# Level products of a gated linear attention: from whole chunks to diagonal blocks in column groups

## The chip, the cores and the metric

One Trainium2 chip, one of its NeuronCores. The metric is the device time of one execution in microseconds (us), lower is better. The kernel computes a whole inference step of a small trunk, and the change touches one part of it, the linear attention.

## The reference, cut to what matters

Layer 0 mixes tokens by bidirectional gated linear attention with 4 heads, 128 key and 256 value channels per head. Within a chunk it is

```python
bcum  = jnp.cumsum(gi, axis=2)                                   # log decay, per token and key channel
diff  = bcum[:, :, :, None, :] - bcum[:, :, None, :, :]
decay = jnp.exp(jnp.where(lower[:, :, None], diff, -jnp.inf))
attn  = jnp.einsum('bhik,bhjk,bhijk->bhij', qi, ki, decay)       # the decay depends on i, j and the channel k
o     = jnp.einsum('bhij,bhjv->bhiv', attn, vi) + ...            # plus the part read from the state
```

once forwards and once on the flipped sequence; the two results are added. There are 1024 latent and 128 context tokens. Around it stand projections, an output projection, a convolutional MLP, and a second layer with Fourier mixing.

## The kernel before, in words

Channels lie on the 128 partitions, the 1152 tokens along the free dimension. The kernel works in chunks of 128 tokens, nine of them, and takes three at a time: 384 columns, here called a **chunk group**. Heads are taken one after the other, and within a head the chunk groups from the last to the first, so `attention` (line 485) runs its loop body (lines 509 to 592) 12 times.

The decay of a pair of tokens depends on the channel, so one product cannot give `attn`. The kernel splits a chunk into **levels** (`LEVELS`, 64 down to 1). At level s the chunk is cut in blocks of 2s tokens, and the product covers pairs whose two tokens lie in different halves of one block, with the decay measured from the middle of the block. For each level POOL and DVE subtract (lines 535 and 537, tile `le`), ACT takes the exponential (540, 544), POOL multiplies with k (541), DVE with q (546), TensorE forms a full product of 128 x 128 for each of the three chunks (549, PSUM tile `lv`), and DVE copies the pairs of this level out of it under a mask (551) into the tile `A`. The pairs of a token with itself come first (527, 528). With the diagonal that makes 24 full products for a chunk group, 288 in all. `A` then goes into the product with v (line 565), which starts the output `o`; after it come the squares and the normalisation (`os`, `ov`, lines 573 to 582).

All these operands are plain fp32: one product stands in the trace as two records, each with its own weight load. The big projections (`pq`, `pk`, `pv`, `pr` for q, k, v and the output gate r, and `wo`, line 621, for the output projection) are split into two fp32r parts and take three records of 256 or 384 columns (lines 97 to 99).

What sets the order: a tile scheduler orders the instructions of each engine ahead of time, by priorities and by its own idea of durations. Each engine then runs its list strictly in that order. While a head's attention runs, the projections of the next head fill TensorE; at the last head there is no next one, and the output projection of heads 0 and 1 (`w_out`) fills instead. `tick` (line 193) puts small pieces of a background job in between, the modulation vectors (`mod_background`, line 175, tile `mods`): products with only 32 stationary columns, four of them side by side in the array's four column groups through `tile_position`. The tiles `le` come from a ring of four buffers, so the levels of the next chunk group are made ahead until the ring is full.

Of the kernel before, what the change touches and what calls it, by code (L numbers as in the profile page):

```python
# [15 lines left out]
F32 = mybir.dt.float32  # L16
# [29 lines left out]
def trunk(tc, a, o):  # L46
# [15 lines left out]
    def t30(name, dt=F32):  # L62
        return sb.tile([P, 2, CH], dt, tag="m3", bufs=4, name=name)
# [4 lines left out]
    def at_ps(name):  # L68
        return pp.tile([P, 512], F32, tag="at", bufs=4, name=name)
# [32 lines left out]
    def const(name, shape, dt=F32, src=None):  # L102
        t = con.tile(shape, dt, name=name)
        if src is not None:
            nc.sync.dma_start(t, src)
        return t
# [273 lines left out]
    gng = const("gng", [P, 2], src=a["gng"])  # L380
    convw = const("convw", [P, 2, 3, NF], src=a["convw"])
    convb = const("convb", [P, 2, NF], src=a["convb"])
    mask = const("mask", [P, len(LEVELS), P], U8)
    mraw = sb.tile([P, 1032], F32, tag="wr", bufs=2, name="mraw")
    nc.sync.dma_start(mraw[:, :len(LEVELS) * P], a["mask"])
    V.tensor_copy(mask.rearrange("p l i -> p (l i)"), mraw[:, :len(LEVELS) * P])
    for ch in range(NCH):
        ev_glr(ch, pss[ch])

# [89 lines left out]
    def kv(kt, v, c):  # L479
# [2 lines left out]
                  start=True, stop=True)  # L482
        return ps

    def attention(h, qk, pages):

        dec = sb.tile([P, 2, 9], F32, tag="dec", bufs=2, name="dec")
# [21 lines left out]
        for cg in (2, 1, 0):  # L509
# [11 lines left out]
                    sbs[c - 1] = s_n  # L521

            att = t15("A")
            ps = at_ps("lv")
            for c in range(3):
                s = cg * CH + c * P
                PE.matmul(ps[:, c * P:(c + 1) * P], lhsT=qk[:, s:s + P], rhs=qk[:, T + s:T + s + P], start=True, stop=True)
            S.activation(att, ps[:, :CH], AF.Copy, scale=2.0)
            for li, s in enumerate(LEVELS):
                nb = CH // (2 * s)  # L530
                base = cg * CH
                e = t30("le")
                ref = view(bb, s - 1, [2 * s, nb], [CH + 1, 2], [0, s])
                if s > 1:
                    G.tensor_tensor(view(e, 0, [2 * s, nb], [s, 2], [1, s]), ref,  # L535
                                    view(bb, 0, [2 * s, nb], [CH + s, 2], [1, s]), op=ALU.subtract)
                V.tensor_tensor(view(e, CH + s, [2 * s, nb], [-s, 2], [1, s]),
                                view(bb, s, [2 * s, nb], [CH - s, 2], [1, s]), ref, op=ALU.subtract)
                if s > 1:
                    S.activation(e, e, AF.Exp, scale=1.0 / TAU)  # L540
                    G.tensor_tensor(e[:, 0], e[:, 0], qk[:, base:base + CH], op=ALU.mult)  # L541
                    kk, kb = e, 0
                else:
                    S.activation(e[:, 1], e[:, 1], AF.Exp, scale=1.0 / TAU)
                    kk, kb = qk, base
                V.tensor_tensor(e[:, 1], e[:, 1], qk[:, T + base:T + base + CH], op=ALU.mult)
                ps = at_ps("lv")
                for c in range(3):
                    PE.matmul(ps[:, c * P:(c + 1) * P], lhsT=view(kk, kb + c * P, [1, P]),  # L549
                              rhs=e[:, 1, c * P:(c + 1) * P], start=True, stop=True)  # L550
                ins = V.copy_predicated(att.rearrange("p (c i) -> p c i", i=P),
                                  mask[:, li, None, :].to_broadcast([P, 3, P]),
                                  ps[:, :CH].rearrange("p (c i) -> p c i", i=P))
                if li % 2 == 0:
                    tick(1, behind=ins)
            qb = t30("qb")
            S.activation(qb, bb.rearrange("p (z i) -> p z i", z=2), AF.Exp, scale=1.0 / TAU)
            V.tensor_tensor(qb, qb, view(qk, T + cg * CH, [0, 2], [1, CH]), op=ALU.mult)
# [999 lines left out]
```

## Time and profile before

| | |
|---|---|
| median of 3 runs (lowest to highest) | 2561.12 us (2558.16 to 2563.42) |
| the profiled execution, its own time | 2564.86 us |
| its span, first to last instruction | 2563.0 us |
| TensorE, matmuls | 2425.1 us busy, 95% |
| VectorE (DVE) | 1841.2 us busy, 72% |
| ScalarE (ACT) | 1089.3 us busy, 43% |
| GpSimd (POOL) | 730.9 us busy, 29% |
| granted TensorE clock, mean | 0.981 of 2.4 GHz |

The attention lies in the first quarter, from about 60 to 660 us. A record of a matmul in the trace is longer than the time that it takes from the next one, since matmuls are pipelined: what counts is the spacing of starts. A granted clock of 1.00 in a row is 2.4 GHz, 0.50 is 1.2 GHz.

### The profile page before, as it was taken

The numbers are of one execution on the slowest core, as the hardware profiler recorded it, in microseconds if no ns is written. First come the engines' busy times: TensorE is split into PE (matmuls) and PEld (weight loads), VectorE is DVE, ScalarE is ACT, GpSimd is POOL, SyncE is SP. The second block draws the span as 40 slices with busy tenths as digits, with TensorE's granted clock in tenths as the row PEclk, the third lists the DMA queues.
The fourth block names the chain that finished last, engine by engine and source line by source line (L and its number), as shares of the span: only waits on it lengthen the run. The fifth ranks groups of instructions, "written<-read, shape, count | busy, mean of one in ns | idle before, by whom it ended". The sixth has DMA issues, their size and how long they took to land. (4 is left out here: it accounts for less than half of the span.)

```text
span 2563.0 us, 46543 instructions
## 1 busy us (share of the span) xinstructions
PE 2425.1 (95%) x18122; PEld 2329.2 (91%) x18122; DVE 1841.2 (72%) x3339; ACT 1089.3 (43%) x2086; POOL 730.9 (29%) x548
## 2 busy tenths in 40 slices
PE   5999999987999999999999998999899999999997
PEld 4998988877999999999999996998899999999997
DVE  7647475566699677777787877277987778778676
ACT  5435344445364323333345564344533333334553
POOL 3435454453202333444100005230144444410000
PEclk8999999998999999999999999999999999999999
DMA  7212222204233453232674357344223232267334
GB/s 263 69 54 89 80 80 82 67 21 146 87 116 124 132 172 104 91 96 83 212 248 135 112 153 216 107 156 144 90 87 117 83 96 87 80 229 224 93 86 125
DMA packets 200972, 309.85 MB, mean 121 GB/s; under 512 B 18288, under 2 KB 142064, under 8 KB 200752
## 3 DMA queue, kind: packets, MB, share of 16 engines
q1 hardware_dynamic: 196528, 302.66, 37.2%
q10 hardware_dynamic: 4224, 4.23, 0.5%
q8 instruction: 142, 2.33, 0.4%
q14 instruction: 78, 0.64, 0.1%
HBM read 233.71 MB, written 73.11 MB: 120 GB/s over the span
## 5 line engine op out<-in xcount | busy, mean ns | idle before, releaser
L98 PE MATMUL pd<-hl,wd 128*128 128x288 f32 x1112 | 328.7, 299 | 5.4 <-DVE hl L1085 5.2
L99 PE MATMUL pd<-hh,wd 128*128 128x288 f32 x1112 | 326.7, 297 | 0.0
L97 PE MATMUL pd<-hh,wd 128*128 128x288 f32 x1112 | 316.5, 298 | 5.5 <-ACT hh L1084 3.2
L809 POOL TENSOR_TENSOR s<-wa,s 128x512 fp32r<-128x512 f32 x114 | 157.0, 1377 | 278.6 <-ACT s L808 278.6
L1084 ACT ACTIVATE hh<-hr 128x288 fp32r<-128x288 f32 x308 | 133.2, 437 | 222.1 <-PE pd L98 213.3
L98 PEld LDWEIGHTS pd<-hl,wd 128*128 128x128 f32 x1112 | 210.8, 190 | 7.9 <-DVE hl L1085 7.4
L1085 DVE TENSOR_TENSOR hl<-hr,hh 128x288 fp32r<-128x288 f32 x308 | 138.5, 455 | 109.3 <-ACT hh L1084 108.7
L97 PEld LDWEIGHTS pd<-hh,wd 128*128 128x128 f32 x1112 | 204.2, 188 | 10.8 <-ACT hh L1084 5.7
L99 PEld LDWEIGHTS pd<-hh,wd 128*128 128x128 f32 x1112 | 210.4, 190 | 0.0
L809 POOL TENSOR_TENSOR a<-wa,a 128x512 fp32r<-128x512 f32 x76 | 100.1, 1318 | 334.7 <-ACT a L808 231.1
L808 ACT ACTIVATE s<-wa 128x512 fp32r<-128x512 f32 x120 | 75.5, 630 | 189.8 <-DVE wa L826 116.1
L977 ACT ACTIVATE hid<-hid 128x576 f32<-128x576 f32 x88 | 60.4, 686 | 161.5 <-DVE hid L972 102.0
L1074 DVE TENSOR_TENSOR wd<-wd,wd 128x512 fp32r<-128x512 f32 (+1 forms) x184 | 116.4, 642 | 9.7 <-ACT wd L1073 4.9
L808 ACT ACTIVATE a<-wa 128x512 fp32r<-128x512 f32 x80 | 50.3, 631 | 141.0 <-PE pa L99 76.2
L1073 ACT ACTIVATE wd<-wd 128x512 fp32r<-128x512 f32 (+1 forms) x184 | 104.4, 580 | 11.7 <-PE ps L99 4.0
L860 DVE TENSOR_TENSOR q<-q,ps 128x288 f32<-128x288 f32 x232 | 98.4, 444 | 10.1 <-PE ps L99 8.4
L535 POOL TENSOR_TENSOR le<-vbr 128x384 f32<-128x384 f32 x72 | 74.0, 1032 | 109.3 <-PE lv L549 95.5
L1208 POOL TENSOR_TENSOR fn<-fn 128x512 f32<-128x512 f32 x8 | 14.1, 1764 | 312.9 <-ACT wp L728 293.3
L541 POOL TENSOR_TENSOR le<-le,qk 128x384 f32<-128x384 f32 x72 | 91.6, 1278 | 35.6 <-ACT le L540 34.7
L97 PE MATMUL pa<-fh1x,a 128*128 128x288 f32 x320 | 95.3, 298 | 5.9 <-DVE c L860 3.6
L97 PE MATMUL ps<-fh1x,s 128*128 128x288 f32 x320 | 95.2, 298 | 3.0 <-DVE hid L917 3.0
L97 PE MATMUL ps<-fh0t,s 128*128 128x288 f32 x320 | 96.4, 302 | 1.4 <-DVE c L860 1.4
(689 smaller groups left out, 8852.5 us busy)
## 6 DMA issues: line engine op xcount, KB each, us to landing
hr<-hid SPq DMA_DIRECT2D x308, 144.0 KB, 2.2
wm<-in_wmod SPq DMA_DIRECT2D x112, 256.0 KB, 2.9
hid<-hid SPq DMA_DIRECT2D x44, 576.0 KB, 3.8
wa<-in_wup SPq DMA_DIRECT2D x40, 512.0 KB, 3.5
wg<-in_wup SPq DMA_DIRECT2D x40, 512.0 KB, 4.1
hid<-t SPq DMA_DIRECT2D x132, 144.0 KB, 3.3
wd<-in_wdn SPq DMA_DIRECT2D x16, 1024.0 KB, 8.0
wm<-in_wmod SPq DMA_DIRECT2D x96, 128.0 KB, 3.5
```

The lines of the kernel that those rows point to most:

```text
L97: PE.matmul(ps, lhsT=wh, rhs=xh, start=first, stop=False, skip_group_check=skip)
L98: PE.matmul(ps, lhsT=wh, rhs=xl, start=False, stop=False, skip_group_check=skip)
L99: PE.matmul(ps, lhsT=wl, rhs=xh, start=False, stop=last, skip_group_check=skip)
L535: G.tensor_tensor(view(e, 0, [2 * s, nb], [s, 2], [1, s]), ref, view(bb, 0, [2 * s, nb], [CH + s, 2], [1, s]), op=ALU.subtract)
L541: G.tensor_tensor(e[:, 0], e[:, 0], qk[:, base:base + CH], op=ALU.mult)
L808: S.activation(w[name][:, :512], x, AF.Copy)
L809: (eng or G).tensor_tensor(w[name][:, 512:], x, w[name][:, :512].bitcast(F32), op=ALU.subtract)
L860: add.last = V.tensor_tensor(out[:, xs], x[:, xs], ps[s][:, :SUB], op=op)
L1073: S.activation(hi, x, AF.Copy)
L1074: low = V.tensor_tensor(lo, x, hi.bitcast(F32), op=ALU.subtract)
L1084: S.activation(hi[:, c], raw, AF.Copy)
L1085: V.tensor_tensor(lo[:, c], raw, hi[:, c].bitcast(F32), op=ALU.subtract)
```

## The change

The level of 64 keeps its full products. The level of 32 is only formed in the two diagonal blocks of 64 of each chunk, the levels of 16 and below and the diagonal only in the four diagonal blocks of 32. Blocks are placed in the column groups of the array by `tile_position`, so that 2 or 4 of them lie side by side. Levels are collected in groups (64; 32 and 16 and the diagonal; 8 and 4; 2 and 1), and the group's products are issued behind the last operand made for it. The small levels gather in a tile `near` of 96 columns, whose blocks are copied into `A` at the end. A chunk group then has 3 products of 128 x 128, 6 of 64 x 64 and 72 of 32 x 32, so 972 products in place of 288. What makes the operands (lines 533 to 546) stays.

```diff
+    def diagonal(ps, n, kk, at, q):
+        for c in range(3):
+            for g in range(P // n):
+                PE.matmul(ps[n * g:n * g + n, c * n:(c + 1) * n], lhsT=view(kk, at + c * P + n * g, [1, n]),
+                          rhs=q[:, c * P + n * g:c * P + n * g + n], start=True, stop=True,
+                          **({} if n == P else dict(tile_position=(0, n * g))))
...
-            for c in range(3):
-                s = cg * CH + c * P
-                PE.matmul(ps[:, c * P:(c + 1) * P], lhsT=qk[:, s:s + P], rhs=qk[:, T + s:T + s + P], start=True, stop=True)
-            S.activation(att, ps[:, :CH], AF.Copy, scale=2.0)
+            att3 = att.rearrange("p (c i) -> p c i", i=P)
+            near = sb.tile([P, 96], F32, tag="near", bufs=2, name="near")
+            todo = []
...
-                V.tensor_tensor(e[:, 1], e[:, 1], qk[:, T + base:T + base + CH], op=ALU.mult)
-                ps = at_ps("lv")
-                for c in range(3):
-                    PE.matmul(ps[:, c * P:(c + 1) * P], lhsT=view(kk, kb + c * P, [1, P]),
-                              rhs=e[:, 1, c * P:(c + 1) * P], start=True, stop=True)
-                ins = V.copy_predicated(att.rearrange("p (c i) -> p c i", i=P),
-                                  mask[:, li, None, :].to_broadcast([P, 3, P]),
-                                  ps[:, :CH].rearrange("p (c i) -> p c i", i=P))
+                made = V.tensor_tensor(e[:, 1], e[:, 1], qk[:, T + base:T + base + CH], op=ALU.mult)
+                todo.append((li, max(2 * s, 32), kk, kb, e[:, 1]))
+                ins = made
+                if li % 2 == 0:
+                    ps = at_ps("lv")
+                    at = 0
+                    with tc.issue_after(made.ins):
+                        for lj, n, kk, kb, q in todo:
+                            diagonal(ps[:, at:], n, kk, kb, q)
+                            at += 3 * n
+                        if li == 2:
+                            diagonal(ps[:, at:], 32, qk, base, qk[:, T + base:T + base + CH])
+                            S.activation(near, ps[:, at:at + 96], AF.Copy, scale=2.0)
+                    at = 0
+                    for lj, n, *_ in todo:
+                        src = ps[:, at:at + 3 * n].rearrange("p (c i) -> p c i", i=n)
+                        at += 3 * n
+                        if n == P:
+                            ins = S.activation(att3, src, AF.Copy)
+                        elif n == 64:
+                            S.activation(att3[:64, :, :64], src[:64], AF.Copy)
+                            ins = V.tensor_copy(att3[64:, :, 64:], src[64:])
+                        else:
+                            ins = V.copy_predicated(near.rearrange("p (c i) -> p c i", i=32),
+                                                    mask[:, lj - 2, None, :].to_broadcast([P, 3, 32]), src)
+                    todo = []
                 if li % 2 == 0:
                     tick(1, behind=ins)
+            for g in range(4):
+                b = slice(32 * g, 32 * g + 32)
+                src = near[b].rearrange("p (c i) -> p c i", i=32)
+                if g % 2:
+                    S.activation(att3[b, :, b], src, AF.Copy)
+                else:
+                    V.tensor_copy(att3[b, :, b], src)
```

The mask shrinks to the blocks of 32 and is built by four copies in place of one.

How the order moves, at three places. In the rows below each line is one product, or with "x3" three alike; the names are tiles (`lv` the level products, `mods` the modulation vectors, `pv`, `pr` and `wo` the projections), and the shape is stationary columns by moving columns. TensorE in head 0, second chunk group, where its level products begin, before:

```order
L527 MATMUL lv<-qk_686 128x128 x3
L549 MATMUL lv<-le 128x128 x4
L186 MATMUL mods_1554<-sel,mrow_1830 128x8
L549 MATMUL lv<-le 128x128 x5
L175 MATMUL mods_1856<-wm_1826,cs 32x128 x4
L175 MATMUL mods_1856<-wm_1828,cs 32x128 x4
L549 MATMUL lv<-le 128x128 x3
```

and now:

```order
L492 MATMUL lv<-le 128x128 x3
L492 MATMUL lv<-le 64x64 x6
L492 MATMUL lv<-le 32x32 x9
L186 MATMUL mods_1578<-sel,mrow_1888 128x8
L492 MATMUL lv<-le 32x32 x3
L492 MATMUL lv<-qk_689 32x32 x12
L492 MATMUL lv<-le 32x32
L175 MATMUL mods_1939<-wm_1884,cs 32x128 x4
L175 MATMUL mods_1939<-wm_1886,cs 32x128 x4
L492 MATMUL lv<-le 32x32 x11
L98 MATMUL pv_1789<-wv10l,h_303 128x256
L492 MATMUL lv<-le 32x32 x12
```

The 12 products of the level of 4 stand behind a projection and not directly behind those of the level of 8; otherwise blocks of one kind stand together. TensorE in the last chunk group of the last head, in the middle of its level products, before:

```order
L549 MATMUL lv<-le 128x128
L97 MATMUL wo_5503<-ot_5150,wo01h 128x384
L549 MATMUL lv<-le 128x128
L98 MATMUL wo_5503<-ot_5150,wo01h 128x384
L549 MATMUL lv<-le 128x128
L99 MATMUL wo_5503<-ot_5150,wo01l 128x384
```

and now:

```order
L492 MATMUL lv<-le 64x64
L98 MATMUL wo_6188<-ot_5676,wo02h 128x384
L492 MATMUL lv<-le 64x64
L99 MATMUL wo_6188<-ot_5676,wo02l 128x384
L492 MATMUL lv<-le 64x64
L97 MATMUL wo_6188<-ot_5679,wo02h 128x384
L492 MATMUL lv<-le 64x64
L98 MATMUL wo_6188<-ot_5679,wo02h 128x384
L492 MATMUL lv<-le 32x32
L99 MATMUL wo_6188<-ot_5679,wo02l 128x384
L492 MATMUL lv<-le 32x32
L97 MATMUL wo_6188<-ot_5684,wo02h 128x384
```

Here single blocks and wide products of the output projection take turns; 58 of this chunk group's blocks stand alone in this way. TensorE after head 0's first chunk group, in the projection `pr`, now:

```order
L97 MATMUL pr_1144<-h_304,wr00h 128x384
L175 MATMUL mods_1578<-wm_1687,cs 32x128
L98 MATMUL pr_1144<-h_304,wr00h 128x384
L175 MATMUL mods_1578<-wm_1687,cs 32x128
L99 MATMUL pr_1144<-h_304,wr00l 128x384
```

Eight `mods` products stand alone there (and at the same place of heads 1 and 2), which before stood in fours and eights further up.

Counted over the whole list, a run of 32- or 64-column products between full-width ones (a **visit** to the narrow shape) occurs 111 times before and 229 times now.

## Rows read from the trace of the kernel before

**Rows 1.** Busy time, clock and DMA by stretch: us, busy (records) per engine.

```profile
core 0: us, PE busy (x) PEld busy (x) DVE busy (x) ACT busy (x) POOL busy (x), PEclk, DMA share, GB/s
60.00:560.00 500.00, 472.49 (x3491) 433.32 (x3490) 296.38 (x464) 218.00 (x385) 226.13 (x172) 0.99 0.23 71
193.10:205.60 12.50, 12.34 (x127) 10.30 (x125) 11.77 (x21) 5.26 (x9) 8.32 (x8) 1.00 0.35 103
597.70:614.80 17.10, 8.63 (x25) 7.12 (x24) 12.53 (x17) 10.29 (x17) 8.96 (x5) 0.50 0.60 214
635.20:651.20 16.00, 16.00 (x111) 15.87 (x109) 13.16 (x23) 4.09 (x7) 4.32 (x4) 1.00 0.01 2
```

**Rows 2.** Timeline, end of head 0's second chunk group: start us, length us, instruction [idle before].

```profile
204.99 0.58 DVE L551 COPY_PREDICATED A<-mask,lv 128x384 f32<-128x384 uint8 x1
...
205.62 0.30 PEld L565 LDWEIGHTS o<-A,vbr 128*128 128x128 f32 x2 [0.29 <-DVE A L551]
```

**Rows 3.** DVE groups of 60 to 660 us by shape: count | busy us, mean ns | idle before.

```profile
L551 DVE COPY_PREDICATED A<-mask,lv 128x384 f32<-128x384 uint8 x84 | 49.2, 586 | 12.5 <-PE lv L549 7.5 <-ACT mrow L184 5.0
...
L461 DVE COPY ns<-kv 128x256 f32<-128x256 f32 x8 | 3.4, 425 | 5.2 <-PE kv L481 5.2
...
L187 DVE TENSOR_TENSOR modT<-mods,bmod 128x8 f32<-128x8 f32 x8 | 1.2, 150 | 0.0
```

**Rows 4.** Timeline of TensorE: level products in a run, then between wide products.

```profile
128.22 2.84 PE L549 MATMUL lv<-le 128*128 128x128 f32 x24
...
641.20 0.38 PE L549 MATMUL lv<-le 128*128 128x128 f32 x2
641.34 0.42 PE L98 MATMUL wo<-ot,wo02h 128*128 128x384 f32 x1
641.60 0.38 PE L549 MATMUL lv<-le 128*128 128x128 f32 x2
...
642.39 0.34 PE L98 MATMUL wo<-ot,wo02h 128*128 128x384 f32 x1
642.57 0.34 PE L99 MATMUL wo<-ot,wo02l 128*128 128x384 f32 x1
```

**Rows 5.** Timeline of TensorE around one visit to the 32-column shape.

```profile
114.62 0.49 PE L474 MATMUL kt<-ident,ke 128*128 128x128 f32 x3
115.03 0.65 PE L175 MATMUL mods<-wm,cs 128*32 128x128 f32 x16
115.61 0.44 PE L97 MATMUL pr<-h,wr00h 128*128 128x384 f32 x1
115.89 0.33 PE L98 MATMUL pr<-h,wr00h 128*128 128x384 f32 x1
```

**Rows 6.** By stretch, as in rows 1: the start of that visit, and a long run.

```profile
115.03:115.06 0.03, 0.03 (x4) 0.03 (x4) 0.00 (x0) 0.00 (x0) 1.00 0.00 0
...
28.00:30.30 2.30, 2.30 (x85) 2.30 (x88) 0.00 (x0) 1.22 (x2) 2.30 (x3) 1.00 1.04 386
```

**Rows 7.** By stretch, then the timeline of TensorE inside the second stretch.

```profile
1553.39:1556.80 3.41, 1.80 (x20) 1.21 (x22) 3.41 (x6) 2.68 (x7) 2.29 (x2) 1.00 0.91 259
1556.80:1563.60 6.80, 6.80 (x37) 4.63 (x36) 6.80 (x9) 2.73 (x10) 4.83 (x5) 0.50 0.96 283
...
1559.20 0.64 PE L175 MATMUL mods<-wm,cs 128*32 128x128 f32 x4
1559.78 0.58 PE L98 MATMUL wp<-dc,fw 128*128 128x258 f32 x1
1560.16 0.42 PE L99 MATMUL wp<-dc,fw 128*128 128x258 f32 x1
1560.50 0.64 PE L175 MATMUL mods<-wm,cs 128*32 128x128 f32 x4
...
1561.46 0.42 PE L98 MATMUL wp<-dc,fw 128*128 128x258 f32 x1
1561.67 0.42 PE L99 MATMUL wp<-dc,fw 128*128 128x258 f32 x1
```

**Rows 8.** Waits of TensorE from 60 to 660 us: total us, times, longest.

```profile
PE ov L577 <- DVE os L575: 10.0, 11, 2.9
PE wo L97 <- ACT wo00h L86: 7.0, 1, 7.0
```

More of the change, by code (lines that the diff above doesn't have):

```diff
@@ L382, in trunk @@
     convb = const("convb", [P, 2, NF], src=a["convb"])
-    mask = const("mask", [P, len(LEVELS), P], U8)
+    mask = const("mask", [P, len(LEVELS) - 2, 32], U8)
     mraw = sb.tile([P, 1032], F32, tag="wr", bufs=2, name="mraw")
     nc.sync.dma_start(mraw[:, :len(LEVELS) * P], a["mask"])
-    V.tensor_copy(mask.rearrange("p l i -> p (l i)"), mraw[:, :len(LEVELS) * P])
+    for g in range(4):
+        b = slice(32 * g, 32 * g + 32)
+        V.tensor_copy(mask[b], mraw[b, 2 * P:len(LEVELS) * P].rearrange("p (l i) -> p l i", i=P)[:, :, b])
     for ch in range(NCH):
@@ L545, in attention @@
                     kk, kb = qk, base
-                V.tensor_tensor(e[:, 1], e[:, 1], qk[:, T + base:T + base + CH], op=ALU.mult)
-                ps = at_ps("lv")
-                for c in range(3):
-                    PE.matmul(ps[:, c * P:(c + 1) * P], lhsT=view(kk, kb + c * P, [1, P]),
-                              rhs=e[:, 1, c * P:(c + 1) * P], start=True, stop=True)
-                ins = V.copy_predicated(att.rearrange("p (c i) -> p c i", i=P),
-                                  mask[:, li, None, :].to_broadcast([P, 3, P]),
-                                  ps[:, :CH].rearrange("p (c i) -> p c i", i=P))
+                made = V.tensor_tensor(e[:, 1], e[:, 1], qk[:, T + base:T + base + CH], op=ALU.mult)
@@ L554, in attention @@
                 if li % 2 == 0:
                     tick(1, behind=ins)
+            for g in range(4):
+                b = slice(32 * g, 32 * g + 32)
+                src = near[b].rearrange("p (c i) -> p c i", i=32)
[3 more added lines that the diff above has]
+                    V.tensor_copy(att3[b, :, b], src)
             qb = t30("qb")
```

## Prediction

> **What bounds the kernel now.** I read the stages first. From 60 to 560 us, where ten of the twelve chunk groups lie, TensorE is busy 472.49 of 500 us at a granted clock of 0.99 [rows 1]; nothing else comes near that over the whole stretch. So work that TensorE sheds or takes on counts there almost in full, unless another engine holds it up in the same place. One does, inside each chunk group: from the first level product to the first product of `o` (193.1 to 205.6 us, 12.5 us) DVE is busy 11.77 us beside TensorE's 12.34 [rows 1], and `o` begins 0.05 us after the end of the last masked copy [rows 2], as it does within 0.15 us in all twelve chunk groups. Inside a chunk group TensorE and the chain over DVE are about equally long, and a gain needs both to become shorter. The last chunk group is different: from 635.2 to 651.2 us TensorE is busy 16.00 of 16.00 us, DVE 13.16 [rows 1]. There TensorE alone sets the pace. Between the last two lies a stage in which TensorE waits 7.0 us for the first weight of the output projection [rows 8], and in which the clock is at 1.2 GHz from 597.7 to 614.8 us with TensorE busy 8.63 of 17.10 us [rows 1].
>
> **Prices.** A level product is two records. In a run 24 records take 2.84 us, the last one's 0.27 included, so (2.84 - 0.27) / 23 = 0.11 us per record; between wide products a pair adds 0.40 - 0.18 = 0.22 us [rows 4]. A chunk group's 24 products cost 24 x 0.22 = 5.3 us.
>
> A visit to the narrow shape has a price of its own. The third `kt` record begins at 114.62 + 0.49 - 0.27 = 114.84 and streams until 114.95. Then come 16 narrow records, four at a time in the four column groups, so 4 x 0.11 = 0.44 us of streaming, and one wide product of 0.17 us, until the next wide one starts at 115.89 [rows 5]. That is 0.94 us, of which 0.61 are streaming: 0.33 us go into emptying the array on the way in and out and into a weight load that isn't hidden. I take 0.33 us for every visit.
>
> The new blocks of 32 columns aren't in this trace. Side by side they need a quarter of a record's 0.11 us for four, 0.007 us each; four narrow records do start within 0.03 us, 0.008 us each [rows 6]. The upper end is what a long run with 128 moving columns sustains, 85 records in 2.30 us, 0.027 us each [rows 6]. I take 0.008, since that run is limited by its 128 moving columns and not by its starts. For the 72 blocks that is 72 x 2 x 0.008 = 1.15 us, or 3.9 us at the upper end.
>
> The Trainium skill speaks against this value: its page "TensorE: Matmul & The Clock Gate", section "Wait — 56ns, not 53.3ns?", says that matmuls never start less than about 25 ns apart, however few columns they have. The four starts within 0.03 us show that this doesn't hold between different column groups. If it held on average over a run, the blocks would cost about what the upper end gives.
>
> **The change, part by part.** *(a) Inside the first ten chunk groups.* Streaming: 3 x 0.22 for the level of 64, 6 x 0.056 for the blocks of 64 (half the columns, two side by side), 0.12 for the step from 64 to 32 columns (an estimate, about a third of a visit), 1.15 for the blocks of 32: 2.3 us in place of 5.3. Visits: these ten stretches have 48 now and 101 in the new order, 24 of which are lone `mods` (b); the other 77 are 2.9 more per chunk group, 2.9 x 0.33 = 1.0 us. TensorE gains 2.0 us. DVE loses seven masked copies of 0.586 us [rows 3], 4.1 us; it gets five copies of 96 columns, one of 192 on half the partitions and two of 96 on a quarter. Their prices lie between 0.15 us (8 columns) and 0.425 us (256 columns) [rows 3]; I take 0.30, 0.35 and 0.25, in sum 2.35 us, so DVE gains 1.75 us (0.7 to 2.9 at the ends). Both chains agree on a little under 2 us: 10 x 1.9 = -19 us, with ends of 0 (blocks of 32 at the upper price) and -29. POOL's subtractions and products stay as they are; ACT gets three or four short copies for one long one, with 218 of 500 us busy [rows 1] to hide them.
>
> *(b) 24 lone `mods` products.* In three places eight of them alternate with projection products. 24 visits x 0.33 = 7.9 us. Each also streams alone, 0.22 us where four side by side take 0.22 together, so 24 x 0.165 = 3.9 us. In sum +11.8 us, in projection stretches where TensorE has the only say.
>
> *(c) The eleventh chunk group and the wait for the first output weight.* All its blocks stand in one visit, and the 18 products of `o` move behind that weight. TensorE idles here anyway, so what it sheds is worth nothing, and 18 x 0.22 = 4 us move onto the path. ACT reaches the weight's split after fewer of the products' successors, which can give back up to the 7.0 us [rows 8]. I take 0, with ends of -8 and +8.
>
> *(d) The last chunk group.* 58 blocks stand alone between wide products. The new order has 64 visits where there was none: 64 x 0.33 = 21.1 us. Streaming is 54 x 0.056 for the lone blocks of 32, 4 x 0.11 for those of 64, and 1.1 for the rest, 4.6 us against 5.3. Being later, TensorE no longer waits at the `ov` product behind it, at most 2.9 us [rows 8]. +17.5 us.
>
> *(e) The clock.* While blocks and wide products alternate, a turn takes 0.17 + 0.33 + 0.06 = 0.56 us, of which the wide product streams 0.17. The trace has a stretch of this kind. From 1553.39 TensorE was busy 1.80 of 3.41 us at full clock; from 1556.8 on the granted clock was 0.50, and it stayed there for 6.8 us although TensorE was busy all the time, for a good part alternating between narrow and wide [rows 7]. At that level a visit costs 1.30 (one turn) - 2 x 0.21 - 2 x 0.215 = 0.45 us [rows 7], and a turn in the last chunk group 0.34 + 0.45 + 0.11 = 0.90 us. If all 58 turns ran so, that were 58 x 0.34 = 20 us; the runs of 13 and 10 wide products between them would add up to 4. I take 13 us, since the stretch begins at the full level and these runs may bring it back, and 2 us for the lone `mods`: +15 us, with ends of 0 and 24.
>
> **The sum** is -19 + 11.8 + 0 + 17.5 + 15 = +25 us. The profiled execution took 2564.86 us (span 2563.0 and 1.9 around it) and would take 2590. It lies 3.7 us above the median of the runs, 2561.12, so the time forecast is 2586 us.
>
> **The rivals.** *The clock holds.* If the alternation of (d) doesn't bring the clock down, (e) falls away: +10 us, 2571. For it: TensorE never waits there. Against it: rows 7, where 6.8 us of alternation without a wait stayed at the lower level. *The small blocks start slowly.* At 0.027 us per record the blocks cost 2.7 us more per chunk group, TensorE's gain in (a) is gone, and DVE's shorter chain doesn't help: +19 on the forecast, 2605. The page's 25 ns would act in this way. For it: no row shows more than a handful of narrow starts in quick succession. *Lone blocks don't pay the full visit; faster.* The price of 0.33 us comes from a visit of 16 records of 128 columns. If a single block of 32 slips between two wide products for the part on the way in alone, about 0.10 us (114.95 to 115.03, and its weights), the 88 visits of (b) and (d) cost 8.8 us in place of 29, (e) falls away, and the sum is -19 + 3.9 + 8.8 - 0.7 - 2.9 = -10 us, 2551. It decides below 0.155 us per visit. Against it: rows 5 show both ways and the open weight load as fixed pieces that don't hang on what is in between. *The products don't stand behind one another.* The order says so for the last chunk group and for the level of 4; that is part of the forecast.
>
> **How the numbers follow.** A difference of 0.2% (5 us) is about what a measurement of this kernel can tell from none. Forecast 0.48, all slower. Clock holds 0.13, of which 0.04 within 0.2% and 0.09 slower. Slow small blocks 0.13, slower. Cheap lone visits 0.14, faster. The remaining 0.12: 0.07 faster (the chain over DVE shrinks by the full 4.1 us, or the wait of (c) goes), 0.05 within 0.2%. Together 0.21 faster, 0.09 the same, 0.70 slower. The range reaches from 2548, so that the faster rival is half in, to 2610 above the slow blocks.
>
> **What would show it.** In the profile after: 32-column records about 0.03 us apart for four; about 0.9 or 0.56 us from one wide product to the next in the last chunk group, with a granted clock of 0.50 over most of it; `o` about 10.5 us behind the first level product in the first ten; the masked copies at 0.3 us. I am wrong if lone blocks stand under 0.4 us from wide to wide, if the clock keeps 1.00 through the last chunk group, or if the last chunk group takes less than 25 us from first level product to `o`.

## The result and the profile after

| | before | after |
|---|---|---|
| median of 4 runs (lowest to highest) | 2561.30 us (2558.16 to 2563.42) | 2606.19 us (2604.65 to 2608.26) |
| span of the profiled execution | 2563.0 us | 2605.4 us |
| granted TensorE clock, mean | 0.981 | 0.973 |
| start of the tenth chunk group's `ov` product | 562.4 us | 580.0 us |
| start of the last product of `wo` | 729.6 us | 770.6 us |

The changed kernel is slower by 1.8%, ratio 1.0177 with a 95% interval of 1.0159 to 1.0194. The two marks in the table split the 42.4 us of span: +17.6 us up to the tenth `ov`, +23.4 us from there to the end of the output projection, +1.4 us in all that follows.

Busy time by stretch, as in [rows 1], first the two stretches of before between these marks:

```profile
core 0: us, PE busy (x) PEld busy (x) DVE busy (x) ACT busy (x) POOL busy (x), PEclk, DMA share, GB/s
60.00:562.40 502.40, 473.25 (x3495) 433.79 (x3493) 298.62 (x466) 218.59 (x386) 227.49 (x173) 0.99 0.23 70
...
562.40:729.60 167.20, 150.90 (x877) 145.60 (x878) 111.87 (x204) 70.93 (x119) 41.66 (x27) 0.94 0.30 104
```

and of after the same two, then a stretch at the lower clock level inside the third chunk group with what stands ahead of it, and the last chunk group from its first level product to `o`:

```profile
60.00:580.00 520.00, 475.78 (x4630) 422.97 (x4628) 311.05 (x479) 225.77 (x426) 227.52 (x173) 0.96 0.22 68
...
580.00:770.60 190.60, 170.25 (x1106) 149.71 (x1107) 108.77 (x206) 70.71 (x125) 41.36 (x27) 0.93 0.27 91
...
231.20:234.60 3.40, 1.96 (x82) 1.55 (x73) 3.40 (x5) 2.16 (x5) 2.99 (x4) 1.00 0.11 10
234.60:241.40 6.80, 5.63 (x99) 4.50 (x99) 5.55 (x11) 1.42 (x3) 3.70 (x4) 0.50 0.28 86
...
664.00:705.50 41.50, 39.86 (x247) 25.12 (x245) 15.78 (x30) 5.51 (x11) 4.05 (x4) 1.00 0.07 23
```

In the first stretch TensorE idles 44.2 us where it idled 29.2: 15.1 of the 17.6 us are waiting, 2.5 are busy time. In the second it is the other way round: busy time grows by 19.4 us, idle time by 4.1. What it waits for now, by the waits of TensorE from 60 to 580 us (total, times, longest):

```profile
PE lv L492 <- DVE le L555: 17.8, 10, 2.6
...
PE mods L175 <- DVE modT L187: 6.9, 7, 1.0
```

The same waits took 2.0 and 0 us before. The level products, which were to become cheaper, now stand waiting for their operands. The DVE groups from 60 to 720 us say why (by shape: count, busy us, mean ns, idle before). First the two operations on `le` in the kernel before, then the same two in the kernel after, and its new masked copies:

```profile
L546 DVE TENSOR_TENSOR le<-le,qk 128x384 f32<-128x384 f32 x84 | 72.1, 870 | 12.4 <-ACT le L540 11.4 <-ACT le L544 0.9
L537 DVE TENSOR_TENSOR le<-vbr 128x384 f32<-128x384 f32 x84 | 63.1, 764 | 11.1 <-PE o L570 11.0
```

```profile
L546 DVE TENSOR_TENSOR le<-vbr 128x384 f32<-128x384 f32 x84 | 89.7, 1081 | 19.1 <-PE o L604 14.1 <-PE lv L492 4.0
L555 DVE TENSOR_TENSOR le<-le,qk 128x384 f32<-128x384 f32 x84 | 78.6, 954 | 6.2 <-ACT le L549 5.5 <-ACT le L553 0.6
L578 DVE COPY_PREDICATED near<-mask,lv 128x96 f32<-128x96 uint8 x60 | 15.5, 258 | 5.2 <-PE lv L492 4.9
```

The copies shrank from 0.586 us [rows 3] to 0.258. But the subtraction and the multiplication, which the change doesn't touch, went from 0.764 and 0.870 us to 1.081 and 0.954. Together that is 33 us more, over the twelve chunk groups, than the same 168 instructions took before, and more than the shorter copies saved (49.2 us against 25.5 for all the copies that took their place). A mean that moves in this way, for one shape, is made of short and long ones. Here is one stretch of the third chunk group, DVE and then POOL:

```profile
234.27 1.36 DVE L555 TENSOR_TENSOR le<-le,qk 128x384 f32<-128x384 f32 x1
235.66 0.36 DVE L576 COPY A<-lv 64x192 f32<-64x192 f32 x1
236.03 0.26 DVE L578 COPY_PREDICATED near<-mask,lv 128x96 f32<-128x96 uint8 x1
236.21 0.55 DVE L555 TENSOR_TENSOR le<-le,qk 128x384 f32<-128x384 f32 x1
236.68 0.26 DVE L578 COPY_PREDICATED near<-mask,lv 128x96 f32<-128x96 uint8 x1
236.84 1.03 DVE L555 TENSOR_TENSOR le<-le,qk 128x384 f32<-128x384 f32 x1
```

```profile
232.83 2.39 POOL L550 TENSOR_TENSOR le<-le,qk 128x384 f32<-128x384 f32 x2 [0.33 <-ACT le L549]
236.48 0.97 POOL L544 TENSOR_TENSOR le<-vbr 128x384 f32<-128x384 f32 x1 [1.26 <-PE lv L492]
```

The multiplication of 236.21 has no POOL instruction beside its start and takes 0.55 us. That of 234.27 takes 1.36: POOL's work ends at 232.83 + 2.39 = 235.22, DVE's at 235.63, 0.41 later. That of 236.84 takes 1.03: POOL ends at 237.45, DVE at 237.87, 0.42 later. In both DVE's end follows POOL's by the same time, whatever DVE's own start was; until POOL ends, DVE counts as busy and gets nothing done. It is so throughout: of the 168 operations on `le`, the 106 that took more than 0.7 us all began during an instruction of POOL, and all ended 0.41 to 0.52 us behind its end. What they took beyond 0.55 us each adds up to 78 us; in the kernel before it is 42 us, in 91 operations with the same distance to POOL's end. The Trainium skill states the rule, which the prediction did not draw on: its page "SBUF — State Buffer", section "SBUF: two separate sides", says that a DVE operation with two SBUF inputs and a GpSimd operation that reads SBUF share one pair of ports, which the first to start holds for its whole instruction while the other stands still. These rows agree: DVE ends 0.41 and 0.42 us behind POOL.

### The profile page after: what moved, and what is told of

The parts are those of the page before. It is cut to its first block, busy times and chain, and to the rows that moved or that the text cites. A ratio compares the mean times of both kernels' runs of the same rounds, so it can differ in the third digit from the quotient of the medians.

```text
span 2605.4 us, 49349 instructions
## 1 busy us (share of the span) xinstructions
PE 2445.6 (94%) x19490; PEld 2318.4 (89%) x19490; DVE 1849.5 (71%) x3354; ACT 1097.2 (42%) x2132; POOL 733.2 (28%) x548
## 5 line engine op out<-in xcount | busy, mean ns | idle before, releaser
L1107 ACT ACTIVATE wd<-wd 128x512 fp32r<-128x512 f32 (+1 forms) x184 | 104.4, 580 | 12.6 <-PE ps L99 4.0
L546 DVE TENSOR_TENSOR le<-vbr 128x384 f32<-128x384 f32 x84 | 89.7, 1081 | 19.1 <-PE o L604 14.1
L550 POOL TENSOR_TENSOR le<-le,qk 128x384 f32<-128x384 f32 x72 | 88.8, 1242 | 44.4 <-ACT le L549 43.7
L894 DVE TENSOR_TENSOR c<-q,pa 128x288 f32<-128x288 f32 x80 | 36.0, 451 | 88.2 <-PE pa L99 82.9
```

Of the source, the lines that this page charges most:

```text
L894: add.last = V.tensor_tensor(out[:, xs], x[:, xs], ps[s][:, :SUB], op=op)
L1107: S.activation(hi, x, AF.Copy)
```

## The experiments

The question for each group of experiments: how much of the 42 us do the lone narrow products cost, is it the grouping or the blocks, and is it DVE and POOL that hold up the chunk groups? The marks are those of the first table; ratios are against the kernel before, run beside each. A mark comes from one execution: nl_mods and nl_last have the same order on TensorE up to the tenth `ov` and reach it at 576.8 and 580.1 us, so differences of 3 us there tell nothing.

| | median us | ratio (95% interval) | tenth `ov` | last `wo` |
|---|---|---|---|---|
| before | | | 562.4 | 729.6 |
| after | 2606.19 | 1.0177 (1.0159 to 1.0194) | 580.0 | 770.6 |
| nl_mods | 2599.44 | 1.0149 (1.0120 to 1.0179) | 576.8 | 766.8 |
| nl_both | 2607.82 | 1.0183 (1.0159 to 1.0208) | 598.4 | 776.4 |
| nl_last | 2580.23 | 1.0064 (1.0042 to 1.0086) | 580.1 | 749.9 |
| groups_only | 2562.29 | 1.0003 (0.9990 to 1.0016) | 563.6 | 729.9 |
| blocks_only | 2605.76 | 1.0171 (1.0145 to 1.0197) | 582.2 | 774.4 |
| pad | 2634.11 | 1.0274 (1.0256 to 1.0291) | 609.1 | 801.4 |
| np_before | 2555.88 | 0.9972 (0.9957 to 0.9986) | 547.6 | 719.7 |
| np_after | 2565.88 | 1.0008 (0.9992 to 1.0024) | 532.8 | 731.4 |
| pk_before | 2582.22 | 1.0083 (1.0065 to 1.0101) | 575.7 | 742.8 |
| pk_after | 2607.92 | 1.0188 (1.0173 to 1.0203) | 584.1 | 775.9 |
| act64 | 2576.08 | 1.0069 (1.0052 to 1.0086) | 573.5 | 746.0 |

**One part alone: groups_only and blocks_only.** The grouping without the blocks leaves the loop's products and copies at full size:

```diff
+                if li % 2 == 0:
+                    with tc.issue_after(made.ins):
...
+                        for lj, kk, kb, q in todo:
+                            ps = at_ps("lv")
+                            for c in range(3):
+                                PE.matmul(ps[:, c * P:(c + 1) * P], lhsT=view(kk, kb + c * P, [1, P]),
+                                          rhs=q[:, c * P:(c + 1) * P], start=True, stop=True)
```

> One part of the change alone: full 128x128 products and full masked copies as in the kernel before, but the levels collected in the four groups, each group's products behind the last operand made for it. 111 visits, as before; no block shape at all. Theory 'grouping makes TensorE wait for operands': about 2 us more per chunk group than before in the first ten, waits of lv for le of 20 us and more, 2580 us or above. Theory 'the masked copies that went away had filled the time of POOL, and DVE's operations on SBUF now collide with POOL': here the copies are back, so DVE's subtraction stays near 0.76 us in the mean, and the time is within 8 us of before, 2561.

The blocks without the grouping, against the changed kernel:

```diff
-                if li % 2 == 0:
+                if True:
                     ps = at_ps("lv")
                     at = 0
-                    with tc.issue_after(made.ins):
+                    with ExitStack():
```

> The other part alone: diagonal blocks in column groups and short copies as in the changed kernel, but each level's products and copies issued as soon as its own operands are made (no groups of levels, no order behind the last operand). 232 visits, 57 lone level blocks in the last chunk group, 24 lone mods. Theory 'visits and the collision of DVE with POOL': as the changed kernel, 2596 to 2610 us, with DVE's subtraction again at 1.0 us and more. Theory 'grouping makes TensorE wait': the first ten chunk groups lose most of their waits for le and gain the 19 us of the forecast, 2580 to 2590 us.

Grouping alone changes nothing: 2562.29 us, DVE's subtraction 0.770 us in the mean, waits of `lv` for `le` 5.9 us. The blocks alone are the whole change: 2605.76 us, the subtraction 0.976 and the multiplication 1.023, waits 14.6 us. The loss lies in the blocks and short copies, not in the waiting for a group's last operand. No run has the short copies without the blocks and the order of before, so these two are not told apart.

**Lone narrow products: nl_mods, nl_both, nl_last.** First the `mods` products (`l == 0` is the first layer):

```diff
-            for g in range(4):
-                PE.matmul(ps[32 * g:32 * g + 32, :P], lhsT=cs[:, k, :], rhs=ws[i][g],
+            with tc.high_priority() if l == 0 else ExitStack():
+                for g in range(4):
+                    PE.matmul(ps[32 * g:32 * g + 32, :P], lhsT=cs[:, k, :], rhs=ws[i][g],
```

> The changed kernel, with the first layer's mods products raised in the scheduler's priority, so that the 24 lone ones of the three places stand in fours and eights again (219 visits in place of 229). All else, the lone level blocks of the last chunk group too, stays. Theory 'a visit has a price': the three places fall back by what they rose, 15.6 us between the ov products around them (11.8 us by the forecast's prices), so 2590 to 2594 us in place of 2606. Rival 'the three places became longer through something else, waits for operands or the shorter chunk groups ahead of them': within 4 us of 2606. In either case the other chunk groups keep their waits for the tile le, and the last chunk group keeps its 41 us.

6.8 us came back where 11.8 to 15.6 were expected. The price itself was right. In the kernel after, lone `mods` between products of `pr` on TensorE:

```profile
149.60 0.44 PE L97 MATMUL pr<-h,wr00h 128*128 128x384 f32 x1
149.97 0.41 PE L175 MATMUL mods<-wm,cs 128*32 128x128 f32 x2
150.30 0.45 PE L98 MATMUL pr<-h,wr00h 128*128 128x384 f32 x1
```

From wide to wide 0.70 us, where two wide ones in a row stand 0.174 apart: 0.53 for a lone block, 24 x (0.53 - 0.055) = 11.4 us for all of them. But the three places only became 2.0 to 3.7 us shorter in nl_mods; moved up, the products lengthen the first chunk group (+3.0 us) and stretches in which TensorE waits anyway, and those waits and the time at the lower clock level stay (16.5 us of `lv` for `le`; 47.8 us at half clock between 60 and 580 us, 44.4 in after, 6.8 before).

Then the level products of the last chunk groups. nl_both raises all of them:

```diff
-                    with tc.issue_after(made.ins):
+                    with tc.high_priority(), tc.issue_after(made.ins):
```

> As nl_mods, and the level products are raised in priority too: no level block stands alone between wide products any more, and the last chunk group has 4 visits in place of 64 (181 visits in all; in the first ten chunk groups the blocks are split into about 3 visits more each). Theory 'a visit has a price': last chunk group -60 x 0.33 = -20 us, lone mods -12 to -16 us, about 30 more visits in the other groups +10 us: 2576 to 2584 us. Rival 'the last chunk group is longer since its operands come late, not since its blocks stand alone': from first level product to o it stays above 30 us, although its blocks stand in runs, and the time stays above 2590. Rival 'operands bound the first ten chunk groups': their waits for le stay or grow, whatever the visits do.

The time did not fall, 2607.82 us, and the theory failed in both parts; the signs of the rival of late operands (above 30 us in the last chunk group, above 2590 us in all) were met. From the tenth `ov` to the last `wo` 178.0 us remain of 190.6, 12.6 less and not 20, although the lone blocks are gone. Ahead of the last chunk group stands a new wait of 12.4 us of `kt` for `ke`, and with it a stretch at half clock,

```profile
638.30:665.60 27.30, 13.58 (x176) 10.35 (x177) 20.73 (x32) 14.27 (x26) 10.75 (x7) 0.50 0.52 177
```

in which TensorE was busy for half of the time. From the first level product to `o` it is still 41.8 us, but what lies between is some 150 records of `wo`, not single blocks. The first ten chunk groups, where the raised products are split up and stand in front of other work, became 18 us longer than in after. So this kernel moves too much to give a price. nl_last raises them in one place only:

```diff
-                    with tc.issue_after(made.ins):
+                    with tc.high_priority() if h == 3 and cg == 0 else ExitStack(), tc.issue_after(made.ins):
```

> nl_mods, with the level products raised in priority in one place only, the last chunk group of the last head. Its lone blocks go into runs (161 visits in all in place of 219), and everything ahead of it keeps its order. Theory 'a lone block between wide products costs a visit': 58 visits at the 0.37 us by which the trace of the changed kernel spaces them are 21.5 us, so the stretch from the tenth ov to the end of the output projection falls from 190.0 us (nl_mods) to 167 to 172, and the time from 2599 to 2576 to 2582. Rival 'the operands of these levels come late anyway, TensorE only waits elsewhere': from first level product to o it stays above 30 us, or a wait of the same size stands behind it; 2592 or above.

That is clean: the order ahead of it is that of nl_mods, and from the tenth `ov` to the last `wo` 169.8 us remain of 190.0, 20.2 less for 58 visits, 0.35 us each; the median is 2580.23. The last chunk group, from first level product to `o`, has gone from 41.5 to 13.7 us:

```profile
664.10:677.80 13.70, 11.70 (x190) 9.36 (x189) 10.63 (x21) 4.85 (x10) 4.05 (x4) 0.88 0.01 1
```

The price was to be read in the kernel after too, since the clock stayed at 1.00 there. TensorE in its last chunk group:

```profile
674.17 0.44 PE L98 MATMUL wo<-ot,wo03h 128*128 128x384 f32 x1
674.54 0.25 PE L492 MATMUL lv<-qk 128*32 128x32 f32 x2
674.72 0.45 PE L99 MATMUL wo<-ot,wo03l 128*128 128x384 f32 x1
675.09 0.25 PE L492 MATMUL lv<-qk 128*32 128x32 f32 x2
675.27 0.44 PE L97 MATMUL wo<-ot,wo03h 128*128 128x384 f32 x1
```

0.55 us from wide to wide (a median of 0.548 over 54 such turns), 0.37 of it for the lone block.

**Is TensorE's spare time free? pad.** Work that nobody needs, put back into nl_mods:

```diff
                         for lj, n, kk, kb, q in todo:
+                            if n < P:
+                                for c in range(3):
+                                    PE.matmul(ps[:, c * P:(c + 1) * P], lhsT=view(kk, kb + c * P, [1, P]),
+                                              rhs=q[:, c * P:(c + 1) * P], start=True, stop=True)
+                        for lj, n, kk, kb, q in todo:
                             diagonal(ps[:, at:], n, kk, kb, q)
```

> nl_mods with work put back on TensorE that nobody needs: ahead of the blocks of each level of 32 and below, the three full 128x128 products of that level are formed as in the kernel before, into the same PSUM tile, where the blocks then overwrite them (levels 32 to 1, 18 products or about 4.0 us per chunk group, 48 us in all). Copies, operands and grouping stay. Theory 'TensorE is what bounds these stretches': 2599 + 40 to 48 = 2640 to 2648. Theory 'the chain over the operands bounds them and TensorE has 3 us to spare': 2597 to 2605, with the waits of lv for le gone. Theory 'what the blocks lose is the clock': the granted clock falls to half for 48 us between 60 and 580 us in nl_mods and for 7 us before; with TensorE kept busy it falls there for less than 15 us, and up to 16 us come back: 2585 to 2597 in spite of the added work.

None of the three: 2634.11 us, 34.7 us more, 32.3 of it up to the tenth `ov` for 10 x 18 x 0.22 = 40 us of products. Time at half clock between 60 and 580 us fell from 47.8 to 23.9 us (to 30.7 up to this kernel's tenth `ov`), the waits of `lv` for DVE's `le` fell to 2.1 us (and 6.9 for POOL's half), and new ones came (`o` for the last copies into `A`, 12.3 us). The added products stand behind a level's last operand and ahead of its copies, on the chain itself, not in the time in which TensorE waits. So the run doesn't say what a product in the waiting time would cost, and the clock's share is not settled by it. It does have full products beside short copies: the two operations on `le` took 148.2 us, against 135.2 in before and 167.1 in nl_mods (subtraction 1.096 us, multiplication 0.689).

**DVE and POOL: np and pk.** np leaves POOL out of the levels, in the kernel before and in nl_mods:

```diff
-                if s > 1:
-                    G.tensor_tensor(view(e, 0, [2 * s, nb], [s, 2], [1, s]), ref,
-                                    view(bb, 0, [2 * s, nb], [CH + s, 2], [1, s]), op=ALU.subtract)
...
-                if s > 1:
-                    S.activation(e, e, AF.Exp, scale=1.0 / TAU)
-                    G.tensor_tensor(e[:, 0], e[:, 0], qk[:, base:base + CH], op=ALU.mult)
-                    kk, kb = e, 0
-                else:
-                    S.activation(e[:, 1], e[:, 1], AF.Exp, scale=1.0 / TAU)
-                    kk, kb = qk, base
+                S.activation(e[:, 1], e[:, 1], AF.Exp, scale=1.0 / TAU)
+                kk, kb = qk, base
```

> The kernel before, with GpSimd (POOL) left out of the levels: its subtraction and its product with k are gone, k goes into the level products undecayed, and ACT's exponential covers half as many columns (part of the computation is left out). DVE and TensorE do all that they did. Theory 'DVE and POOL slow each other on SBUF': DVE's subtraction and multiplication fall from 0.76 and 0.87 us to 0.55 to 0.65; the time falls by a little, 2545 to 2560, since TensorE was almost fully busy. Theory without such a collision: they stay within 0.05 us.

> The same left out of nl_mods (blocks in column groups, no lone mods). Theory 'the saved work of TensorE and DVE was lost to DVE and POOL colliding': DVE's subtraction and multiplication fall from 1.08 and 0.94 us to 0.55 to 0.65, the waits of lv for le between 60 and 580 us from 16.5 to under 6 us, and the first ten chunk groups become 10 to 25 us shorter than in np_before, as the forecast wanted. Theory 'the loss lies in the blocks themselves or in the order': the first ten chunk groups stay 10 us or more longer than in np_before. The last chunk group has 81 lone blocks here, so the total says little; the tenth ov is what counts.

In np_before the subtraction and the multiplication fell to 0.616 and 0.548 us, and the tenth `ov` came 14.8 us earlier than in before. Without POOL the change does in the first ten chunk groups what the forecast said. The tenth `ov` of np_after stands at 532.8 us, 14.8 ahead of np_before; from the first to the tenth `ov` it is 386.4 against 402.6 us, 16.2 us or 1.8 per chunk group, and up to there no matmul of a level stands waiting for DVE's `le`. (The whole of np_after is slower than np_before all the same, since lone blocks stand in its last chunk group too, 42.7 us from first level product to `o`.) The DVE groups of np_after from 60 to 720 us:

```profile
L544 DVE TENSOR_TENSOR le<-vbr 128x384 f32<-128x384 f32 x84 | 51.3, 624 | 46.5 <-PE o L597 38.9 <-PE lv L493 7.0
L548 DVE TENSOR_TENSOR le<-le,qk 128x384 f32<-128x384 f32 x84 | 45.9, 554 | 4.4 <-ACT le L546 3.0
```

and its third chunk group, first level product to `o`:

```profile
221.80:230.10 8.30, 8.27 (x220) 7.01 (x219) 7.94 (x21) 4.86 (x13) 0.00 (x0) 1.00 0.34 97
```

8.3 us where the kernel after needs 13.6, with DVE again busy for nearly all of it. But removing POOL also removes the wait for its values, and in the kernel after the weight loads do wait for these (19.9 us from 60 to 580 us). pk puts its work back beside, with nobody waiting for the result:

```diff
                 V.tensor_tensor(view(e, CH + s, [2 * s, nb], [-s, 2], [1, s]),
                                 view(bb, s, [2 * s, nb], [CH - s, 2], [1, s]), ref, op=ALU.subtract)
+                S.activation(e[:, 1], e[:, 1], AF.Exp, scale=1.0 / TAU)
                 if s > 1:
-                    S.activation(e, e, AF.Exp, scale=1.0 / TAU)
                     G.tensor_tensor(e[:, 0], e[:, 0], qk[:, base:base + CH], op=ALU.mult)
...
+                kk, kb = qk, base
```

> np_before with GpSimd's work put back beside it: POOL subtracts and multiplies into its half of the tile le as in the kernel before, but nothing of TensorE or ACT reads that half (k goes into the level products undecayed; part of the computation is left out). So POOL is busy as before and nobody in a level waits for its values. Theory 'DVE and POOL slow each other': DVE's subtraction and multiplication go back from 0.62 and 0.55 us to 0.75 to 1.0, the tenth ov from 547.6 us towards 555 to 563. Theory 'what counted was the wait for POOL's values': they stay at 0.62 and 0.55, the tenth ov stays at 546 to 550.

> The same on nl_mods (blocks in column groups, no lone mods): POOL works beside, nobody in a level waits for its values. Theory 'DVE and POOL slow each other': DVE's subtraction and multiplication are at 0.9 to 1.1 us again, most of the 14.8 us by which the tenth ov of np_after (532.8) stood ahead of that of np_before (547.6) is gone, and it stands within 6 us of that of pk_before or behind it. Theory 'what counted was the wait for POOL's values': the tenth ov stays at 530 to 538, 10 us or more ahead of pk_before's.

The tenth `ov` went to 584.1 us with the blocks and to 575.7 without them: the gain of 14.8 has become a loss of 8.4. From the first to the tenth `ov` it is 428.5 against 423.0 us, 5.5 more where np had 16.2 less. The DVE groups of pk_after, and TensorE's longest wait from 60 to 580 us:

```profile
L547 DVE TENSOR_TENSOR le<-vbr 128x384 f32<-128x384 f32 x84 | 92.8, 1119 | 32.0 <-PE o L602 27.4 <-PE lv L493 3.7
L553 DVE TENSOR_TENSOR le<-le,qk 128x384 f32<-128x384 f32 x84 | 73.6, 886 | 3.3 <-ACT le L549 2.3
...
PE lv L493 <- DVE le L553: 16.8, 10, 2.8
```

The same instructions are back at 1.119 and 0.886 us. 105 of them are longer than 0.7 us, each ending 0.41 to 0.52 us behind a POOL instruction, where np_after has 4. TensorE waits for DVE's `le` as long as in nl_mods (16.5 us), though nobody waits for POOL's values, and no idle time of DVE is ended by POOL, so it is not the ring of `le` tiles, whose slots POOL's half also holds, that delays it. pk_before was slower than expected (575.7 in place of 555 to 563): of the 13.3 us by which it is behind the kernel before, 7.2 lie ahead of the first `ov` already (152.7 against 145.5 us). Why is not shown; its operations on `le` take only 4.8 us more.

**Taking load off DVE and POOL: act64.** The level of 64 gets its exponentials of differences from ACT:

```diff
+                if s == 64:
+                    rb = sb.tile([P, 2, 2, 3], F32, tag="rb", bufs=2, name="rb")
+                    for i in range(2):
+                        S.activation(rb[:, i], view(bb, s - 1, [CH + 1, 2], [P, 3]), AF.Copy, scale=(1 - 2 * i) / TAU)
+                    for b in range(nb):
+                        for z in range(2):
+                            for i, at in enumerate((z * (CH + s), s + z * (CH - s))):
+                                S.activation(e[:, i, b * P + s * (z ^ i):b * P + s * (z ^ i) + s],
+                                             view(bb, at + b * P, [1, s]), AF.Exp, scale=(2 * i - 1) / TAU,
+                                             bias=rb[:, i, z, b:b + 1])
```

> nl_last, with the level of 64 taken off DVE's and POOL's subtraction: ACT forms the exponential of the difference itself, block by block with the reference as its bias (12 short exponentials and 2 copies of 6 columns per chunk group in place of one long exponential; one subtraction of DVE and one of POOL fewer). Everything else stays. Theory 'DVE and POOL colliding is what the shed work was lost to': DVE loses a subtraction of 1.1 us and about 0.5 us of collision per chunk group, 12 x 1.0 to 1.6 = 12 to 19 us: 2561 to 2570 us, the first ten chunk groups 10 to 16 us shorter than in nl_last (580.1 at the tenth ov). Rival 'the tail of copies and the waiting in a fixed order bound the chunk group, whatever DVE carries': within 5 us of 2580. Rival 'ACT becomes the bound' (its 14 short instructions at about 0.22 us against 0.84): above 2580.

The first ten chunk groups became 6.6 us shorter than in nl_last, where 10 to 16 were expected, and the time of 2576.08 us misses the theory's 2561 to 2570 and lies within the 5 us of the rival that the copies and the fixed order bound the chunk group. The multiplication on DVE rose from 0.934 to 1.055 us, so part of what was taken away came back as blocking, and the short exponentials took 0.336 us each in place of 0.22. The ratio to before, 1.0069 against nl_last's 1.0064, shows no gain. So act64 gives the theory no support beyond the np and pk runs, and leaves that rival open as a further limit. No kernel with the whole computation beats the one before.

## Why the prediction was right and wrong

Slower was right, and 2606 lies in the range; the forecast was 20 us too low, and two of its terms were far off in opposite directions. That the time fell in the range is in part luck: (a) missed by some 25 us one way and (e) by 13 us the other. It is luck, too, that the rival of slow small blocks names 2605 us, since its mechanism is refuted below.

- **What bounds the kernel.** That a gain needs both TensorE and DVE to become shorter was right. The step that failed was to read DVE's 11.77 busy us of 12.5 [rows 1] as work. About 2.2 us of it are DVE standing behind POOL, by what the operations on `le` there took beyond 0.55 us; POOL was busy 8.32 us in that stretch. In the same chunk group of after it is 4.9 us of 12.8: 2.7 us more blocking, where the forecast had DVE gain 1.75.
- **Prices.** All held roughly. A lone block costs 0.37 us with its own streaming, where 0.33 + 0.06 = 0.39 was forecast; putting one into a run saved 0.35 us in nl_last. The masked copies take 0.258 us for 0.30. 32-column blocks in a run start 0.008 us apart: 22 records span 0.37 us, one alone 0.20, and (0.37 - 0.20) / 21 = 0.008. So the rival of slow small blocks is out, and the 25 ns of the Trainium skill's page "TensorE: Matmul & The Clock Gate", section "Wait — 56ns, not 53.3ns?", don't hold on average over a run in several column groups either. The two rows, on TensorE in the third chunk group after:

```profile
231.79 0.20 PE L492 MATMUL lv<-le 128*32 128x32 f32 x1
...
233.50 0.37 PE L492 MATMUL lv<-le 128*32 128x32 f32 x22
```

- **Term (a), -19 us.** This failed. Its mechanism exists, since without POOL the change brings 1.8 us per chunk group (1.9 was forecast). With POOL, what DVE's copies no longer take is lost again to blocking: the copies read PSUM and ran at 0.586 us beside POOL's instructions (0.589 in np_before, without POOL). With the copies shortened, the operations on SBUF move up into that time and stand still there; this step is argued from the rows, no run shortens the copies alone. TensorE's saved products turned into waits. With them came 37.6 us more at half clock up to 580 us, as in the row of 234.6 to 241.4 us, ahead of which TensorE was busy 1.96 of 3.40 us. Waits alone did not bring this in pk_before, with full products (TensorE idle for 42.2 us from 60 us to the tenth `ov`, against 44.2 in after, and 6.8 us at half clock), nor did blocks alone in np_after (20.2 us idle, 6.8 at half clock). Blocking costs time without the clock, too: from the first to the tenth `ov` pk_before takes 423.0 us where np_before takes 402.6, with 6.8 and 3.4 us at half clock from 60 us on. How much of the +17.6 us is the one and how much the other is open. TensorE's busy time up to the tenth `ov` rose by 2.5 us where (a) and (b) had it fall by 8.2, so 10.7 us are to be explained; 37.6 us more at half clock cost at most half of that, 18.8, which would be enough.
- **Term (b), +11.8 us.** Right in place, 11.4 us by the spacing of starts. But only 6.8 us come back when the lone products no longer stand alone, since nl_mods puts them elsewhere.
- **Terms (c) and (d), 0 and +17.5 us.** Right in sum. nl_last takes 58 visits away and 20.2 us go; with 169.8 against 167.2 us before, only 2.6 remain for all else in that part. The parts of (c) came out otherwise: the wait of 7.0 us for the first output weight [rows 8] is gone, but level products wait longer for their operands behind the tenth `ov` of after:

```profile
PE lv L492 <- DVE le L555: 11.8, 3, 6.9
```

- **Term (e), +15 us.** This failed where it was put: through the 41.5 us of the last chunk group the clock kept 1.00, with TensorE busy 39.86 us. The rival "the clock holds" was right there. The row it was built on [rows 7] begins with 1.80 us busy of 3.41, and that idle time came ahead of the fall; the alternation alone did not bring the clock down here. It fell in the first ten chunk groups instead, where TensorE waited and where the forecast had taken 2 us, for the lone `mods`.
- **What would show it.** 0.56 us from wide to wide and 0.03 us for four records came about; `o` 10.5 us behind the first level product did not (11.7 to 13.6 us). The condition "wrong if the clock keeps 1.00 through the last chunk group" was met.

Of the three numbers that matter, (d) was near, (e) was 13 us too high in its place, and (a) was 19 us too optimistic, with some 6 us of waits and clock on top (17.6 - 11.4).

## What to carry to other kernels

An engine's busy time can hold another engine's time: before counting on a chain over DVE to shrink, look at how far durations of one shape spread (here 0.55 to 1.37 us for the multiplication) and what POOL does in the long ones. Shortening the copies, which POOL did not hold up, brought nothing here, since operations that it does hold up moved into their place; and with TensorE's order fixed, its saved work returned as waits and time at the lower clock. Narrow blocks side by side in column groups are as cheap as their columns, but one between two wide products costs 0.37 us, so their order must be controlled, at the one place where it goes wrong.

## What the runs showed of the hardware

- A DVE operation with two SBUF inputs that began during a POOL operation and took more than 0.7 us ended 0.41 to 0.52 us behind POOL's end, in 106 of 106 cases of after; alone it takes 0.55. Copies from PSUM did not lengthen (0.586 us beside POOL, 0.589 without it).
- Alternating single narrow and wide products for 41.5 us, with TensorE busy 39.86 us of it, left the granted clock at 1.00.
